# Three kinds of small DMA leave SyncE's queue for ScalarE's and GpSimd's in a two-branch streaming attention layer

## The chip, the cores and the metric

The kernel runs on one core of one Trainium2 chip. The metric is the device time of one execution in microseconds (us); the time of a kernel is the median of its runs. The engines are written as in the profile: PE is TensorE (matmuls; PEld its weight loads), DVE is VectorE, ACT is ScalarE, POOL is GpSimd, SP is SyncE. SP, ACT and POOL can issue DMAs, each from its own queue of instructions, which it works off in order. Each engine waits at an instruction until what it needs from others is there, and what stands behind that instruction on the same engine waits too.

## The reference

One layer of a streaming encoder for 2048 prompt rows and 8 x 16 sample rows (with 512 cached positions each), in float32. Two token mixers work side by side on the same normalised and modulated rows `h`:

```python
qa, ka, va, za, qb, kb, vb, zb, ga, gb = split(h @ w_in)     # 1024 -> 6144
qa, ka = rope(qa), rope(ka)                                  # branch A: 4 heads x 2 x 64
w  = softmax(qa1 ka1') - lam * softmax(qa2 ka2')             # differential attention, chunk-causal mask
oa = w @ va
z  = qb kb' / 8                                              # branch B: 8 heads x 64
a  = sigmoid(z) * exp(reverse exclusive cumsum of log sigmoid(-z))   # stick-breaking attention
ob = a @ vb
ya = (rms_norm(oa) * silu(za)) @ w_branch_a;  yb = (ob * silu(zb)) @ w_branch_b
y  = rms_norm(x + gate * ((sigmoid(ga) * ya + sigmoid(gb) * yb) @ w_out))
```

Besides y for both groups of rows, the outputs are the new keys (of A after rotation) and values of both branches.

## The kernel before

Rows are worked in 17 tiles of 128: prompt tiles 0 to 15 and the sample tile, which the code calls `t == NT`. Products run in float16 pairs: a number is split into a high and a low half, and three of the four products are added up. The work has three stages.

*Start* (to about 200 us in the trace): the modulation, the norm, and `h` transposed, kept in DRAM as `hT_d`.

*Streaming* (to about 1800 us): eight units, alternately a head of A and a pair of heads of B (`kind` 0 and 1). For each unit, `project` (L407) runs over the 17 tiles: 24 matmuls (L428) of the tile's `h`, which SP loads one step ahead (L405), against the unit's weights. `finish` (L438) then evacuates the result. In branch A ACT copies it to `pr` (L442); POOL rotates q and k in three operations (L469, L471, L474) with cosines and sines from a small table `rope`, which `start` (L413) loads for the tile (L423); ACT and DVE split q, k and v into halves. Then come the stores of the tile's k (L484: `rot` in A, `pr` in B), its v (L485) and, in A, of z (L488). `scores` (L625) makes the scores of one tile of queries against all tiles before it. In A the softmax pair is exponentials on ACT and combinations on DVE (L558, L603). In B ACT makes sigmoids, DVE a running product from the right (the scan, L616), POOL multiplies the two (L622, in `stick_weights`), and `turn` (L565) lets ACT write the high half (L572) and DVE the low half (L573; in A L290 and L295). SP then turns the weights with a DMA transpose (L580) into `wt`. Two steps later `pv` (L703) multiplies `wt` with the values (L696 to L698 in A, L700 and L701 in B). `natural` (L669) evacuates the sum to the tile `o`: in A one ACT operation (L675), in B one of ACT (L680), one of DVE (L681) and, for prompt tiles, one of POOL (L683). `store` (L686) adds up the squares of an output of A on ACT (L272) and stores `o` to `o_d[t]` in DRAM (L690).

Into these steps the code interleaves projections for later tiles (about five steps ahead), preparation of the next unit's weights, and norms of caches and weights loaded for that only (L848).

*End* (from about 1800 us): `inputs` (L1168) loads `o_d`, `z_d` and `g_d` tile by tile for the two branch products, the merge and the output product; attention of the sample rows runs beside it and ends in the same `natural` and `store`.

Before the change nearly every DMA is issued by SP (`load` is SP's `dma_start`); ACT issues nine small loads at the start and POOL none. The order of instructions on each engine is not that of the code: the framework lays it out when the program is built, by a simulated timeline of all engines and queues (`schedule_with_timeline_sim=True`), and the chip works it off as laid out. The pools that matter here: `rope`, `rot` and `o` have two buffers each, `wt` five.

Of the kernel before, what the change touches and what calls it, by code (L numbers as in the profile page):

```python
# [25 lines left out]
P = 128  # L26
# [6 lines left out]
NT = SEQ // P  # L33
# [76 lines left out]
def layer_kernel(ctx: ExitStack, tc: tile.TileContext, a: dict):  # L110
    nc = tc.nc
    V, S, G, T = nc.vector, nc.scalar, nc.gpsimd, nc.tensor
    load = nc.sync.dma_start
# [43 lines left out]
    def out_rows(name, t, lo, n):  # L157
        p, s = outs[name]
        return p[t * P : (t + 1) * P, lo : lo + n] if t < NT else s[:, lo : lo + n]
# [3 lines left out]
    o_d = [dram.tile([P, D], F32, name=f"o_d{t}") for t in range(NT + 1)]  # L163
# [23 lines left out]
    def bank(tag, dt=F32):  # L187
        return ps.tile([P, 512 if dt == F32 else 1024], dt, tag=tag, name=f"ps_{tag}", bufs=BANKS[tag])
# [78 lines left out]
    def sum_squares(src, n, dst, width=1024, scale=1.0):  # L267

        for i in range(0, n, width):
            junk = tiny.tile([P, width], F16, tag="junk", name="junk", bufs=1)  # L270
            w = min(width, n - i)
            S.activation(out=junk[:, 0:w], in_=src[:, i : i + w], func=AF.Square, scale=scale,  # L272
                         accum_out=dst[:, i // width : i // width + 1])
# [13 lines left out]
    def split(hi, lo, src, s, on=None):  # L287

        if on is S:
            S.activation(out=hi, in_=src, func=AF.Identity, scale=s)  # L290
        elif on is G:
            G.tensor_scalar(out=hi, in0=src, scalar1=s, scalar2=0.0, op0=ALU.mult, op1=ALU.add)
        else:
            V.tensor_scalar(out=hi, in0=src, scalar1=s, scalar2=None, op0=ALU.mult)
        V.scalar_tensor_tensor(out=lo, in0=src, scalar=s, in1=hi, op0=ALU.mult, op1=ALU.subtract)  # L295
# [106 lines left out]
    def fetch_h(u, t):  # L402
        ahead[u, t] = hs[len(fetched) % 3].bitcast(F16).rearrange("p (f k n) -> p f k n", f=2, n=P)
        fetched.append(t)
        load(out=ahead[u, t], in_=hT_d[t // 4][:, t % 4, :, :, :])  # L405

    def project(U, t):  # L407

        kind, h, sc, sq = U["kind"], U["h"], U["sc"], U["sq"]
        g, i = t // 4, t % 4  # L410
        box = {}

        def start():  # L413
            if t in at_hand:
                box["h"] = at_hand.pop(t)
            else:
                if (U["u"], t) not in ahead:
                    fetch_h(U["u"], t)
                box["h"] = ahead.pop((U["u"], t))
            box["p"] = bank("mm")  # L420
            if kind == 0:
                box["r"] = stg.tile([P, 96], F32, tag="rope", name="rope")
                load(out=box["r"], in_=a["shapes"][:, t * 96 : t * 96 + 96])  # L423

        def mm(n):
            hi, wi = ((0, 0), (0, 1), (1, 0))[n % 3]
# [3 lines left out]
        def piece(n):  # L430
            if n == 0:
                start()
            for j in range(2 * n, 2 * n + 2):
                mm(j)
            if n == 11:
                finish()

        def finish():  # L438
            p, s2, s = box["p"], sc[:, 2:3], sq[:, 0:1]
            pr = stg.tile([P, 512], F32, tag="pr", name="pr", bufs=3)  # L440
            if kind == 0:
                S.activation(out=pr, in_=p, func=AF.Identity, scale=sc[:, 1:2])  # L442
            elif t == NT:
                S.activation(out=pr[:, P:512], in_=p[:, P:512], func=AF.Identity, scale=sc[:, 1:2])
            else:
                S.activation(out=pr[:, P:384], in_=p[:, P:384], func=AF.Identity, scale=sc[:, 1:2])

                assert t % len(rings) not in silu_z
                silu_z[t % len(rings)] = rings[t % len(rings)]
                S.activation(out=rings[t % len(rings)], in_=p[:, 384:512], func=AF.Identity, scale=sc[:, 1:2])  # L450

            qb = qbuf[t % len(qbuf)]
            k16 = stg.tile([P, 2, 2, 64], F16, tag="k16", name="k16")
            vt = kvp.tile([P, 2, 2, 64], F16, tag="v", name="v", bufs=V_BUFS)

            def halves(dst, src, scale):
                src = src.rearrange("p (c d) -> p c d", d=64)
                split(dst[:, :, 0, :], dst[:, :, 1, :], src, scale, S)

            def query(src, scale):  # L460
                src = src.rearrange("p (c d) -> p c d", d=64)
                S.activation(out=qb[:, 0, :, :, :], in_=src.unsqueeze(2).to_broadcast([P, 2, 2, 64]), func=AF.Identity, scale=scale)
                V.scalar_tensor_tensor(out=qb[:, 1, :, 0, :], in0=src, scalar=scale, in1=qb[:, 0, :, 0, :], op0=ALU.mult, op1=ALU.subtract)  # L463
            if kind == 0:
                cosT, sinT = box["r"][:, 0:32], box["r"][:, 32:96]
                x4 = pr[:, 0:256].rearrange("p (c f d) -> p c f d", c=4, f=2)
                rot = stg.tile([P, 256], F32, tag="rot", name="rot")
                r2 = stg.tile([P, 256], F32, tag="r2", name="r2", bufs=1)
                G.tensor_tensor(out=rot.rearrange("p (c f d) -> p c f d", c=4, f=2), in0=x4,  # L469
                                in1=cosT.unsqueeze(1).unsqueeze(1).to_broadcast([P, 4, 2, 32]), op=ALU.mult)  # L470
                G.tensor_tensor(out=r2.rearrange("p (c f d) -> p c f d", c=4, f=2), in0=x4[:, :, ::-1, :],  # L471
                                in1=sinT.rearrange("p (f d) -> p f d", f=2).unsqueeze(1).to_broadcast([P, 4, 2, 32]),
                                op=ALU.mult)
                G.tensor_tensor(out=rot, in0=rot, in1=r2, op=ALU.add)  # L474
                halves(vt, p[:, 256:384], s2)
                query(rot[:, 0:128], s)
                halves(k16, rot[:, 128:256], s)
            else:
                rot = pr
                halves(vt, p[:, 256:384], s2)  # L480
                halves(k16, p[:, 128:256], s2)
                query(p[:, 0:128], s2)
            nk, nv = ("ak", "av") if kind == 0 else ("bk", "bv")
            load(out=out_rows(nk, t, h * P, P), in_=rot[:, 128:256])  # L484
            load(out=out_rows(nv, t, h * P, P), in_=pr[:, 256:384])  # L485
            ui = (h + 4 * kind) * P
            if kind == 0 or t == NT:
                load(out=z_d[t][:, ui : ui + P], in_=pr[:, 384:512])  # L488
            U["v"][t] = vt
            if t == NT:  # L490
                load(out=s_d[U["u"]][:, 6:8, :], in_=vt.rearrange("p c f d -> p c (f d)"))
            U["q16", t], U["k16", t] = qb, k16
# [193 lines left out]
    def store(U, t, o):  # L686
        ui = (U["h"] + 4 * U["kind"]) * P
        if U["kind"] == 0:
            sum_squares(o, P, osums[:, t, U["h"] : U["h"] + 1])
        load(out=o_d[t][:, ui : ui + P], in_=o)  # L690

    def pv_block(job, seg, po, wj, vt, first, last):

# [9 lines left out]
    def pv(job):  # L703

        U, t, c = job["U"], job["t"], job["c"]
        segs = job["segs"] if U["kind"] == 0 else job["segs"][::-1]
        order = [(seg, j) for seg in segs for j in range(seg["hi"] - seg["lo"])]

        def block(i):
            seg, j = order[i]  # L710
            if i == 0 and (U["kind"] == 0 or c == 0):
                U["po", t] = bank("o")
            pv_block(job, seg, U["po", t], j, U["v"][seg["lo"] + j], i == 0, i == len(order) - 1)
            if i == len(order) - 1 and (U["kind"] == 0 or c == 1):
                store(U, t, natural(U, t, U.pop(("po", t))))

        return [(1.5, lambda i=i: block(i)) for i in range(len(order))]
# [4 lines left out]
    def sample(U, dec, qpad, cs):  # L722
# [85 lines left out]
        def finish():  # L808
            po = bank("s")
            vn = box["s"][:, 6:8, :].rearrange("p c (f d) -> p c f d", f=2)  # L810
            for job in box["jobs"]:
                pv_block(job, job["segs"][0], po, 4, vn, True, True)
            o = natural(U, t, po, dec)
            pt = bank("t")
            T.transpose(pt[:, 0:P], box["ot"], ident)
            V.tensor_tensor(out=o, in0=o, in1=pt[:, 0:P], op=ALU.add)
            store(U, t, o)
# [430 lines left out]
    for n in range(len(steps) + PV_LAG):  # L1248
        made, qk, vs = [], [], []
        if n < len(steps):  # L1250
            u, t = steps[n]
# [175 lines left out]
```

## Time and profile before

| | us |
|---|---|
| median of 3 runs | 2351.17 (2347.64 to 2351.97) |
| the profiled execution | 2338.96 |
| its span, first to last instruction | 2337.1 |
| granted TensorE clock in it, mean | 0.965 |
| PE / DVE / ACT / POOL busy | 2121.6 / 1707.5 / 1663.1 / 661.3 |

A row of the profile that names an instruction gives its source line, engine, operation and the tiles it writes and reads (`out<-in`). In the table of waits, `PE ps_o L700 <- DMA wt<-sc_n` reads: PE stood idle before its instruction of L700, which writes `ps_o`, until a DMA from `sc_n` to `wt` had landed; then come the total in us, how often, and the longest. An engine's letter with a `q` (SPq, ACTq) is its sequencer issuing a DMA; its duration is the issue, not the transfer. In the timeline a row begins with start and duration in us, and a bracket holds the idle time before it. The table of stretches gives the length, the busy time of PE, PEld, DVE, ACT and POOL with the number of their instructions, the granted clock, the busy share of the DMA engines and GB/s.

### The profile page before, as it was taken

What the parts mean: (1) busy time and instruction counts of PE and PEld (TensorE: products, weight loads), DVE (VectorE), ACT (ScalarE), POOL (GpSimd) and SP (SyncE); (2) the same over time, 40 slices, a digit from 0 to 9 for tenths busy, and PEclk for the clock granted to TensorE, in tenths of its full rate; (3) what the DMA queues carried; (4) which work ended last, traced back from release to release, by engine and by line L of the source; (5) the groups of instructions that cost most, each with busy time, mean ns of one, the idle gap of its engine ahead of it and who ended that gap; (6) DMA issues with size and microseconds to landing.
All of it is one profiled execution on the core that took longest, in us unless ns stands there. A gap on an engine that the chain in (4) does not pass through costs nothing. (4 is left out here: it accounts for less than half of the span.)

```text
span 2337.1 us, 42708 instructions
## 1 busy us (share of the span) xinstructions
PE 2121.6 (91%) x15272; PEld 1144.0 (49%) x15272; DVE 1707.5 (73%) x3653; ACT 1663.1 (71%) x3292; POOL 661.3 (28%) x578
## 2 busy tenths in 40 slices
PE   5998898998989899899999979999995878989998
PEld 3654454545545445445545545554553444544443
DVE  4658765779875677978667797777788777777663
ACT  4968777787877778778677777866777656756541
POOL 1222022356300334731024474103345111121111
PEclk7999999999999999999999999999997988999999
DMA  9777659897895898867577777756677999999521
GB/s 333 275 214 180 152 118 272 179 193 168 212 210 126 216 204 192 179 178 192 134 191 176 185 168 186 195 146 150 146 171 166 285 254 233 257 245 236 155 98 53
DMA packets 834358, 445.35 MB, mean 191 GB/s; under 512 B 537210, under 2 KB 777130, under 8 KB 833632
## 3 DMA queue, kind: packets, MB, share of 16 engines
q1 hardware_dynamic: 833196, 442.24, 76.0%
q8 instruction: 119, 1.95, 0.4%
q14 instruction: 95, 0.78, 0.1%
q10 hardware_dynamic: 948, 0.39, 0.1%
HBM read 245.60 MB, written 69.24 MB: 135 GB/s over the span
## 5 line engine op out<-in xcount | busy, mean ns | idle before, releaser
L622 POOL TENSOR_TENSOR sc_p<-sc_p,sc_n 128x127 f32<-128x127 f32 (+7 forms) x192 | 313.8, 1638 | 826.5 <-DVE sc_n L616 812.2
L428 PE MATMUL ps_mm<-wb,hs 128*128 128x512 f16 x1632 | 414.5, 382 | 1.5 <-DMA hs<-hT_d 1.3
L428 PEld LDWEIGHTS <-hs 128*128 128x128 f16 x3120 | 274.4, 98 | 257.3 <-DMA hs<-hT_d 11.8
L428 PE MATMUL ps_mm<-wa,hs 128*128 128x512 f16 x1488 | 374.6, 382 | 9.8 <-DVE qbuf L463 6.4
L616 DVE TENSOR_TENSOR_SCAN sc_n<-ps_s,sc_n,zero_t 128x512 f32<-128x512 f32 x192 | 245.4, 1278 | 68.4 <-ACT ps_s L119 65.0
L639 PE MATMUL ps_s<-k,qst 128*128 128x512 f16 (+3 forms) x640 | 224.2, 351 | 37.9 <-DVE sc_n L616 29.9
L573 DVE TENSOR_TENSOR sc_n<-sc_p,sc_n 128x128 f16<-128x128 f32 (+7 forms) x192 | 212.7, 1112 | 58.1 <-ACT sc_n L572 57.6
L504 PEld LDWEIGHTS <-hs 128*128 128x128 f16 x1632 | 156.6, 98 | 188.3 <-ACT qst L532 6.2
L119 ACT ACTIVATE sc_p<-ps_s,usc 128x512 f32<-128x512 f32 (+3 forms) x320 | 204.8, 640 | 30.2 <-PE ps_s L640 25.3
L640 PE MATMUL ps_s<-k,qst 128*128 128x512 f16 (+3 forms) x640 | 224.2, 352 | 0.0
L572 ACT CAST sc_n<-sc_p 128x128 f16<-128x128 f32 (+7 forms) x192 | 155.5, 813 | 78.5 <-POOL sc_p L622 76.9
L700 PE MATMUL ps_o<-v,wt 128*128 128x128 f16 x1088 | 171.5, 225 | 32.6 <-DMA wt<-sc_n 32.2
L119 ACT ACTIVATE ps_s<-ps_s,usc 128x512 f32<-128x512 f32 (+3 forms) x328 | 200.0, 610 | 0.0
L504 PE MATMUL ps_t<-wa,hs 128*128 128x512 f16 x816 | 192.9, 383 | 7.6 <-ACT qst L532 6.0
L504 PE MATMUL ps_t<-wb,hs 128*128 128x512 f16 x816 | 191.9, 380 | 1.2 <-DVE qst L532 0.8
L1344 PE MATMUL ps_o<-wo,wb 128*128 128x512 f16 x816 | 186.5, 383 | 4.1 <-ACT wb L1166 4.1
L701 PE MATMUL ps_o<-v,wt 128*128 128x64 f16 x1088 | 157.9, 197 | 0.0
L700 PEld LDWEIGHTS <-wt 128*128 128x128 f16 x1088 | 105.1, 101 | 98.1 <-DMA wt<-sc_n 45.1
L558 DVE TENSOR_SCALAR_CACHE_REDUCE sc_p<-ps_s,usc 128x512 f32<-128x512 f32 (+3 forms) x160 | 106.3, 665 | 42.4 <-PE ps_s L640 31.7
L616 DVE TENSOR_TENSOR_SCAN sc_n<-ps_s,zero_t 128x128 f32<-128x128 f32 (+3 forms) x128 | 104.1, 814 | 44.0 <-ACT ps_s L119 43.4
L558 DVE TENSOR_SCALAR_CACHE_REDUCE sc_n<-ps_s,usc 128x512 f32<-128x512 f32 (+3 forms) x160 | 106.3, 665 | 36.9 <-PE ps_s L640 26.3
L701 PEld LDWEIGHTS <-wt 128*128 128x128 f16 x1088 | 103.1, 100 | 54.3 <-issue 1.1
(360 smaller groups left out, 4493.6 us busy)
## 6 DMA issues: line engine op xcount, KB each, us to landing
hs<-hT_d SPq DMA_DIRECT2D x130, 512.0 KB, 4.2
g_d<-gt SPq DMA_DIRECT2D x68, 256.0 KB, 4.2
wb<-g_d SPq DMA_DIRECT2D x26, 512.0 KB, 4.8
out_dram<-pr SPq DMA_DIRECT2D x204, 64.0 KB, 2.3
o_d<-o SPq DMA_DIRECT2D x136, 64.0 KB, 2.2
hs<-o_d SPq DMA_DIRECT2D x17, 512.0 KB, 5.6
out_dram<-x SPq DMA_DIRECT2D x17, 512.0 KB, 2.8
wide<-in_w_ada_dram SPq DMA_DIRECT2D x8, 1024.0 KB
```

What stands on the lines that cost most here:

```text
L119: i = S.activation(**kw)
L428: T.matmul(box["p"], box["h"][:, hi, k, :], U["w"][k][:, wi, :], start=(n == 0), stop=(n == 3 * KT - 1))
L504: T.matmul(box["g"][:, 0:gw], box["h"][:, hi, k, :], U["wg"][k // per][:, k % per, wi, :], start=(j == 0), stop=(j == 3 * KT - 1))
L558: V.tensor_scalar(out=dst[:, lo : lo + n], in0=p[:, 0:n], scalar1=sc_pos, scalar2=None, op0=ALU.mult, op1=ALU.max, accum_out=job["mx"][:, ...
L573: V.tensor_tensor(out=lo, in0=src, in1=hi, op=ALU.subtract)
L616: V.tensor_tensor_scan(out=dst[:, lo : lo + n][:, ::-1], data0=src[:, 0:n][:, ::-1], data1=zero_t[:, 0:1].to_broadcast([P, n]), initial=fi ...
L622: G.tensor_tensor(out=p[:, 0:m], in0=p[:, 0:m], in1=n[:, 1 : m + 1], op=ALU.mult)
L639: T.matmul(p[:, 0:n], qst[:, c, :], kk[:, c, 0:n], start=True, stop=False)
L640: T.matmul(p[:, 0:n], qst[:, 2 + c, :], kk[:, c, 0:n], start=False, stop=not diag)
L700: T.matmul(po[:, c * P : (c + 1) * P], wt[:, wj, :], vt[:, c, :, :], start=first, stop=False)
L701: T.matmul(po[:, c * P : c * P + 64], wt[:, nb + wj, :], vt[:, c, 0, :], start=False, stop=last)
L1344: T.matmul(po, st["y"][:, yi * 8 + k, :], wo[j * 4 + k // 2][:, wi, k % 2, :], start=(n == 0), stop=(n == 3 * KT - 1))
```

## The change

Three kinds of DMA are issued by other engines; what they copy, and all computation, stays.

- The load of the rotation table of a tile in branch A (L423), 68 in all, is issued by POOL.
- The store of the rotated k of branch A (L484 with `rot`), 68 in all, is issued by POOL. The k of B and all v and z stay with SP.
- The store of a unit's output `o` (L690) is issued by ACT in branch A (64) and by POOL in branch B (64). The 8 of the sample tile stay with SP.

```diff
             if kind == 0:
                 box["r"] = stg.tile([P, 96], F32, tag="rope", name="rope")
-                load(out=box["r"], in_=a["shapes"][:, t * 96 : t * 96 + 96])
+                G.dma_start(out=box["r"], in_=a["shapes"][:, t * 96 : t * 96 + 96])
...
             nk, nv = ("ak", "av") if kind == 0 else ("bk", "bv")
-            load(out=out_rows(nk, t, h * P, P), in_=rot[:, 128:256])
+
+            (G.dma_start if kind == 0 else load)(out=out_rows(nk, t, h * P, P), in_=rot[:, 128:256])
             load(out=out_rows(nv, t, h * P, P), in_=pr[:, 256:384])
...
         if U["kind"] == 0:
             sum_squares(o, P, osums[:, t, U["h"] : U["h"] + 1])
-        load(out=o_d[t][:, ui : ui + P], in_=o)
+        queue = load if t == NT else S.dma_start if U["kind"] == 0 else G.dma_start
+        queue(out=o_d[t][:, ui : ui + P], in_=o)
```

## The prediction

> **What bounds the kernel now.** I read the page's first part, then TensorE's (PE's) waits, then SyncE's (SP's) own waits and issues, then stretches of the timeline, and last the stages. The profiled execution took 2338.96 us, 1.86 us more than its span; the median of the runs shown is 2351.17 us, 12.2 us above it. I work the change out in us of the span and put it on the median.
>
> ```profile
> span 2337.1 us, 42708 instructions
> PE 2121.6 (91%) x15272; PEld 1144.0 (49%) x15272; DVE 1707.5 (73%) x3653; ACT 1663.1 (71%) x3292; POOL 661.3 (28%) x578
> ```
>
> PE is busy in 91% of the span, so the kernel is bound by PE wherever PE has work, and a gain must be idle time of PE. What ends that idle time and has to do with a DMA is mostly `wt`, the weights turned by a DMA transpose (L580) that SP issues:
>
> ```profile
> PE ps_o L700 <- DMA wt<-sc_n: 32.2, 25, 4.8
> PE ps_o L696 <- DMA wt<-sc_n: 20.4, 14, 4.2
> PE ps_s L639 <- DVE sc_n L616: 29.9, 43, 2.5
> ```
>
> The columns are us in total, times, longest. PE waits 52.6 us in 39 places for `wt`; that is the ceiling of what a freer SP can give by this road (2.3%). The third row is the scan of VectorE (DVE) in branch B, which no queue changes.
>
> SP is one queue in order. Its issues, with duration in ns (min/median/max):
>
> ```profile
> L580 SPq DMA_TRANSPOSE wt<-sc_n x288: 1167/1768/5439, 148.1 to 1798.6; - x144
> L423 SPq DMA_DIRECT2D rope<-in_shapes_dram x68: 332/422/1771, 42.7 to 1471.3; - x68
> L484 SPq DMA_DIRECT2D out_dram<-rot x68: 337/382/1213, 65.9 to 1489.5; - x68
> L690 SPq DMA_DIRECT2D o_d<-o x136: 319/386/3044, 157.9 to 2222.9; - x136
> SPq L690 <- ACT o L675: 34.8, 19, 6.4
> SPq L690 <- POOL o L683: 30.8, 20, 4.9
> SPq L484 <- POOL rot L474: 16.0, 18, 2.4
> ```
>
> 288 transposes by 1.77 us hold SP for about 509 us. The moved copies are 68 tables, 68 rotated k and 128 of the 136 outputs (the sample tile's 8 stay): 68 x 0.42 + 68 x 0.38 + 128 x 0.39 = 104 us of issue. And SP stood 81.6 us at their makers (last three rows) with everything behind it held. So the queue is loaded, but most of its load stays.
>
> **What leaves SP's queue.** How much of PE's 52.6 us hangs on the moved copies I took from the timeline: for each of the 39 waits I went back to the transpose that ended it, took the time from the end of the DVE instruction that made its data to its issue, and in that stretch the moved copies with the waits ahead of them. In 13 of the 39 there was one. The first, one in the middle with three, and the last:
>
> ```profile
> 204.74 0.45 SPq L690 DMA_DIRECT2D o_d<-o  x1
> 205.28 3.37 SPq L580 DMA_TRANSPOSE wt<-sc_n  x1
> 210.83 0.29 PE L696 MATMUL ps_o<-v,wt 128*128 128x128 f16 x1 [2.22 <-DMA wt<-sc_n]
> ...
> 657.67 1.28 DVE L295 SCALAR_TENSOR_TENSOR sc_n<-sc_p,r,sc_n 128x1024 f16<-128x1024 f32 x1
> 659.75 0.51 SPq L690 DMA_DIRECT2D o_d<-o  x1
> 661.42 1.17 SPq L423 DMA_DIRECT2D rope<-in_shapes_dram  x1
> 664.70 0.40 SPq L690 DMA_DIRECT2D o_d<-o  x1
> 665.19 3.84 SPq L580 DMA_TRANSPOSE wt<-sc_n  x2
> 670.11 0.23 PE L696 MATMUL ps_o<-v,wt 128*128 128x128 f16 x1 [1.98 <-DMA wt<-sc_n]
> ...
> 1794.48 1.21 DVE L573 TENSOR_TENSOR sc_n<-sc_p,sc_n 128x1024 f16<-128x1024 f32 x1
> 1796.46 4.40 SPq L580 DMA_TRANSPOSE wt<-sc_n  x2
> 1800.95 0.29 PE L700 MATMUL ps_o<-v,wt 128*128 128x128 f16 x1 [4.85 <-DMA wt<-sc_n]
> ```
>
> At 204.74 one output (0.45 us and the gaps) stands before the transpose: 0.54 us earlier without it. In the middle the data were there at 658.95, the transposes went out at 665.19, and three moved copies took 2.33 us of that; PE waited 1.98, so 1.98 counts. Taking in each place the smaller of the two, the 13 give 8.9 us (0.05 to 1.98 each, the last 0.67). In the other 26 the data themselves were late, or other transposes, loads and stores stood in front. So this term is **-8.9 us**, if each transpose lands as much earlier as it is issued earlier; it is 0 if landing is held by the transfers before it, and no more than -52.6.
>
> **ScalarE's (ACT's) queue** takes 64 outputs of A. Each is issued behind L675, which makes the tile, and the sum of squares that reads it, both ACT's own, so it waits for no other engine. ACT issued copies before only at the start:
>
> ```profile
> L958 ACTq DMA_DIRECT2D wide<-in_lambda_q_dram x2: 352/538/723, 2.7 to 3.7; - x2
> 620.00:900.00 280.00, 262.43 (x1789) 140.19 (x1788) 193.86 (x416) 216.04 (x465) 60.64 (x56) 0.99 0.81 188
> 1010.00:1290.00 280.00, 268.65 (x1830) 143.78 (x1829) 200.41 (x463) 209.71 (x458) 67.63 (x65) 0.99 0.73 176
> 1410.00:1690.00 280.00, 270.62 (x1859) 145.89 (x1858) 211.66 (x497) 200.78 (x445) 71.35 (x71) 1.00 0.66 165
> ```
>
> The last three rows are the stretches that hold most of branch A (columns after the length: PE, PEld, DVE, ACT, POOL busy, clock, DMA share, GB/s). At SP's 0.39 us the 64 cost 25 us of ACT, at a transpose's 1.77 us (an issue held behind one) 113 us. ACT is idle 64 + 70 + 79 = 213 us in these three stretches, while PE is at 94 to 97%. Behind an issue stand ACT's evacuations and exponentials; their lateness is hidden by that idle time, so I take **0**, and 25 us would be the price with the cover gone. A gain is excluded: ACT only gets work.
>
> **GpSimd's (POOL's) queue** takes 200: 68 tables, 68 rotated k, 64 outputs of B. None waits for another engine's compute: L474 and L683 make the k and the output on POOL itself, and the table's buffer is freed by L471, also POOL's. What changes is that a table's load now stands behind whatever POOL waits at, and that L622 (A's rotations too) stands behind issues:
>
> ```profile
> POOL sc_p L622 <- DVE sc_n L616: 812.2, 143, 97.0
> ACT sc_n L572 <- POOL sc_p L622: 76.9, 75, 3.6
> DVE sc_n L573 <- ACT sc_n L572: 57.6, 50, 3.9
> 500.00:620.00 120.00, 109.54 (x817) 60.09 (x816) 110.04 (x218) 96.25 (x207) 73.56 (x64) 0.99 0.81 183
> 900.00:1010.00 110.00, 97.31 (x776) 53.76 (x774) 96.31 (x162) 88.51 (x183) 64.61 (x52) 1.00 0.83 184
> 1290.00:1410.00 120.00, 106.79 (x832) 58.55 (x831) 104.59 (x153) 96.10 (x189) 67.63 (x50) 0.99 0.80 177
> ```
>
> Of the 192 L622, 143 begin when the scan lets them: an issue ahead of these falls into POOL's idle time and is free. 49 (26%) do not. From L622 the lateness goes to ACT's L572 and, in 50 of 192 cases (26%), on to DVE, which is 87 to 92% busy in the three stretches of the last rows, the ends of a B unit with the next unit's A projections beside them. By their places on SP, 74 of the 200 copies fall there (32, 24 and 18; tables, k and outputs by the timeline). 74 x 0.26 x 0.26 = 5.0 issues reach DVE. No row shows what POOL's issue takes. From below it is SP's 0.39 us: 2.0 us; from above a transpose's 1.77 us: 8.9 us, or 20 us if not 26% but POOL's busy share of these stretches, 205.8 of 350 us (59%), is hit (74 x 0.59 x 0.26 = 11.4 issues). I take **+2.0**, as the moved copies' own rows (same tile, same bytes) are the nearest. In the stretches of A above POOL is 22 to 26% busy and hides its part.
>
> The table's load has a price of its own where it comes to stand behind the same waiting L622 as the rotation that reads it. Then POOL waits for a landing:
>
> ```profile
> rope<-in_shapes_dram SPq DMA_DIRECT2D x68, 48.0 KB, 2.4
> ```
>
> 28 tables fall into the three B ends: 28 x 2.4 x 0.26 = 17 us if all did and a quarter reached DVE. The table has two buffers and is loaded at a projection's first piece, its rotation follows the last, so I take 0.
>
> The Trainium skill speaks against POOL's part: its page "SBUF — State Buffer", section "SBUF: two separate sides", says that GpSimd writes the descriptors of its DMAs itself and can't while VectorE runs an op in a mode that holds the port they share. DVE's long rows here are scans out of PSUM and ops of two tensors, which the same page does not count among the modes, so by this rule I would add nothing; no DMA of POOL is in this trace to test it.
>
> **The sum** is -8.9 + 0 + 2.0 = -6.9 us: 2344 us on the median. About 0.2% (4.7 us) is what a measurement of this kernel can tell from no change, so the step is just outside. Its own range is 2338 to 2347.
>
> **The rivals.**
> - *Hidden anyway* (no change, 2347 to 2355). The moved copies only make room in which the transposes wait for each other, or for a landing. For it: the transposes alone are 509 us of issue, and 26 of the 39 waits have no moved copy in front. With half of the 8.9 us realised and the 2.0 paid, it is -2.4: 2349 us. The Trainium skill, "DMA: Bandwidth & Descriptors", section "Issuing engines are not separate DMA queues", states that all queues run on the same DMA engines and that several issuers save only issue time, usually small; by it this rival would be the rule.
> - *GpSimd becomes the late link* (slower). Place: the three B ends above. Price: 11.4 issues x t; at 1.77 us 20 us, less the 8.9 gained: +11, 2362 us, or 2371 with nothing gained. From t = 0.78 us it eats the gain, from 1.2 us the kernel is slower by over 0.2%. Against it: POOL's idle time there is 46.4, 45.4 and 52.4 us, into which 32, 24 and 18 issues fit up to 1.45, 1.9 and 2.9 us each.
> - *A larger gain.* SP's order is not the code's but laid out beforehand from an estimated timeline:
>
> ```profile
> 999.52 0.53 SPq L485 DMA_DIRECT2D out_dram<-pr  x1
> 1002.56 0.38 SPq L484 DMA_DIRECT2D out_dram<-rot  x1
> ```
>
> In the code L484 comes first. With 264 copies gone the layout of every queue is new. If half of the 52.6 us goes, that is -26: 2325 us. The new layout can also lose: PE is idle 38 us in the three stretches of A and 36 in the three B ends, and a fifth more of these 75 us is +15, with the -6.9 it is +8: 2359 us.
>
> **How the numbers follow.** Forecast 0.38, larger gain 0.14, hidden 0.25, GpSimd late 0.16, a worse layout 0.07. Faster by over 0.2%: 0.38 + 0.14 = 0.52; within: 0.25; slower: 0.16 + 0.07 = 0.23. The range goes from 2320 (most of the larger gain) to 2365 (most of GpSimd's price); I leave out about 0.1 on each side.
>
> **What would show it.** Right: SP's waits at L690 for ACT and POOL (65.6 us) and at L484 for POOL (16.0) gone; PE's waits for `wt` down from 52.6 to about 44 us; ACT's waits for L622 not over 85 us; POOL's issues under 0.8 us. Wrong: POOL's issues over 1 us with ACT's and DVE's waits behind L622 up by tens of us; PE's waits for `wt` unchanged although SP is freer; a new wait of POOL's L471 for its table; or differences spread over all engines without a link to the moved copies, which would be the layout.

## The result and the profile after

The kernel after takes 2362.96 us (median of 7 runs, 2355.45 to 2368.18), the kernel before beside it 2347.64 (7 runs, 2342.01 to 2352.07): a ratio of 1.0061 with a 95% interval of 1.0047 to 1.0076. The change makes the kernel slower by 0.6%, 15 us; forecast was 2344 us and faster, the range reached to 2365. The profiled execution after took 2366.43 us, near its median; that of before (2338.96) lies 9 us under its own, so the two profiles differ by 27 us where the medians differ by 15.

The first part of the page after, span and busy times:

```profile
span 2364.6 us, 42426 instructions
PE 2132.6 (90%) x15272; PEld 1150.4 (49%) x15272; DVE 1714.0 (72%) x3653; ACT 1663.8 (70%) x3292; POOL 761.1 (32%) x778
```

POOL has 200 instructions more and is busy 100 us longer: its issues count as work, about 0.5 us each. The queues (packets, MB, share of 16 engines):

```profile
q1 hardware_dynamic: 795180, 426.03, 73.7%
q0 software_dynamic: 6400, 12.01, 2.0%
q10 hardware_dynamic: 10164, 4.58, 0.8%
```

About 16 MB have gone from SP's q1 to q0 (POOL) and q10 (ACT). The moved issues, with ns min/median/max and first and last start (the diff adds one line above L485 and another above L690; before's L484 and L690 are L485 and L692 here):

```profile
L423 POOL DMA_DIRECT2D rope<-in_shapes_dram x68: 545/590/712, 1.3 to 1470.3; - x68
...
L485 POOL DMA_DIRECT2D out_dram<-rot x68: 537/540/586, 67.0 to 1489.7; - x68
...
L692 ACTq DMA_DIRECT2D o_d<-o x64: 326/326/362, 158.7 to 1592.6; - x64
L692 POOL DMA_DIRECT2D o_d<-o x64: 537/578/588, 336.6 to 1821.1; - x64
```

POOL's issue takes 0.54 to 0.59 us, below the 0.78 us that the prediction set as its limit. PE's longest waits after:

```profile
PE ps_o L702 <- DMA wt<-sc_n: 37.5, 23, 7.0
PE ps_o L698 <- DMA wt<-sc_n: 26.3, 19, 3.2
PE ps_s L640 <- DVE sc_n L617: 21.6, 32, 2.9
PE ps_t L805 <- DMA dwt<-dsc: 19.9, 4, 11.1
```

The waits for `wt` (first two rows) are 63.8 us where before had 52.6 and the forecast 44. The last row, from the attention of the sample rows in the end stage, has doubled (9.5 us before), and no moved copy lies there. SP's waits after:

```profile
SPq L581 <- DVE sc_n L574: 128.3, 60, 7.7
...
SPq L486 <- ACT v L290: 72.0, 37, 7.0
...
SPq L485 <- ACT pr L446: 58.8, 24, 6.6
```

and the same three before:

```profile
SPq L580 <- DVE sc_n L573: 74.5, 51, 4.0
...
SPq L484 <- ACT pr L446: 41.6, 19, 6.0
...
SPq L485 <- ACT v L290: 40.5, 28, 5.7
```

SP's waits for the makers of `rot` and `o` are gone, as foretold. In their place SP stands longer for the data of its transposes and stores: 259 us in these three rows where it was 157. It arrives earlier and finds nothing to send. ACT's wait behind L622, which the prediction's slower rival wanted up by tens of us, went down:

```profile
ACT sc_n L573 <- POOL sc_p L623: 68.8, 55, 4.1
```

### The profile page after: what moved, and what is told of

The parts are those of the page before. It is cut to its first block, busy times and chain, and to the rows that moved or that the text cites. A ratio compares the mean times of both kernels' runs of the same rounds, so it can differ in the third digit from the quotient of the medians.

```text
span 2364.6 us, 42426 instructions
## 1 busy us (share of the span) xinstructions
PE 2132.6 (90%) x15272; PEld 1150.4 (49%) x15272; DVE 1714.0 (72%) x3653; ACT 1663.8 (70%) x3292; POOL 761.1 (32%) x778
## 3 DMA queue, kind: packets, MB, share of 16 engines
q8 instruction: 119, 1.95, 0.4%
## 5 line engine op out<-in xcount | busy, mean ns | idle before, releaser
L623 POOL TENSOR_TENSOR sc_p<-sc_p,sc_n 128x127 f32<-128x127 f32 (+7 forms) x192 | 305.4, 1593 | 766.4 <-DVE sc_n L617 760.4
L428 PE MATMUL ps_mm<-wa,hs 128*128 128x512 f16 x1488 | 369.8, 380 | 5.3 <-DMA hs<-hT_d 3.0
L617 DVE TENSOR_TENSOR_SCAN sc_n<-ps_s,sc_n,zero_t 128x512 f32<-128x512 f32 x192 | 245.6, 1279 | 68.3 <-ACT ps_s L119 64.2
L574 DVE TENSOR_TENSOR sc_n<-sc_p,sc_n 128x128 f16<-128x128 f32 (+7 forms) x192 | 218.2, 1141 | 48.5 <-ACT sc_n L573 48.3
L573 ACT CAST sc_n<-sc_p 128x128 f16<-128x128 f32 (+7 forms) x192 | 155.3, 810 | 69.4 <-POOL sc_p L623 68.8
L1346 PEld LDWEIGHTS <-wb 128*128 128x128 f16 x816 | 79.7, 100 | 107.3 <-issue 14.4
```

What stands on the lines that cost most here:

```text
L428: T.matmul(box["p"], box["h"][:, hi, k, :], U["w"][k][:, wi, :], start=(n == 0), stop=(n == 3 * KT - 1))
L573: S.copy(out=hi, in_=src)
L574: V.tensor_tensor(out=lo, in0=src, in1=hi, op=ALU.subtract)
L617: V.tensor_tensor_scan(out=dst[:, lo : lo + n][:, ::-1], data0=src[:, 0:n][:, ::-1], data1=zero_t[:, 0:1].to_broadcast([P, n]), initial=fi ...
L623: G.tensor_tensor(out=p[:, 0:m], in0=p[:, 0:m], in1=n[:, 1 : m + 1], op=ALU.mult)
L1346: T.matmul(po, st["y"][:, yi * 8 + k, :], wo[j * 4 + k // 2][:, wi, k % 2, :], start=(n == 0), stop=(n == 3 * KT - 1))
```

## The experiments

**How order and queue were taken apart.** The framework lays out every engine's order anew when a queue changes. Counted in the two traces, at 6567 of the 15272 places in PE's row of matmuls another one stands after the change (by line, tiles and shape), and at 2077 of DVE's 3653. So nearly all kernels below are built twice: once with one set of queues, to read the order of every engine, SP's other DMAs included; then with another set, each instruction tied behind its predecessor in the first order on its engine, without a wait. Only the moved copies find their places freely. In short form:

```diff
+    nc, _, _, names = built(first)
+    order = [(x.name, x.engine) for b in nc.m.functions[0].blocks for x in b.instructions if x.name in names]
+    nc, arrays, _, names = built(second, order)
...
+                    if str(x.engine) in last:
+                        tc.add_manual_dep(x, last[str(x.engine)], NOSYNC, reason="order")
+                    last[str(x.engine)] = x.name
```

Ratios are to before on the same chip, with 95% intervals. F and T (False and True) say whether a kind moves, in the order tables, rotated k, outputs of A, outputs of B. The traces of the tied kernels show the tied order on every engine. The method by itself, in pin_self:

```diff
+    built([F, F, F, F]); built([F, F, F, F], order)
```

> The kernel before, its own order fixed by the same edges as in the other kernels of this kind, nothing moved: the same program by both theories, 0.9992 to 1.0008. Anything outside is the method's own error, and every ratio of this kind is then read against it.

It gave 0.9994 (0.9981 to 1.0008): no change.

**Queues or order?** Two kernels each keep one half of the change.

pin_queues: before's order, after's queues.

```diff
+    built([F, F, F, F]); built([T, T, T, T], order)
```

> All 264 copies go through the new queues, but every other instruction of every engine stands in exactly the order that it has in the kernel before. Theory Q (the new queues themselves cost the time: GpSimd's issues ahead of its products, ScalarE's ahead of its evacuations): about +14 us on before, as the whole change. Theory L (the queues are worth the few us that were forecast, and the rearranged order of all engines costs the time): -3 to -9 us on before.

pin_layout: after's order, all copies with SP.

```diff
+    built([T, T, T, T]); built([F, F, F, F], order)
```

> The reverse: all copies stay with SyncE, but every engine's other instructions stand in the order of the changed kernel. Theory L: +14 to +24 us on before (the whole loss, and without what the queues give). Theory Q: within 3 us of before.

The queues alone gave 1.0038 (1.0024 to 1.0053), the order alone 1.0024 (1.0009 to 1.0039). Together that is 0.62%, the whole 0.61%: the halves add up, and each is a loss. So neither theory came true: Q wanted the whole with the queues, L a gain there.

**Which order?** Outputs alone were moved with the order left to the framework, then that order was kept and the copies put back on SP.

outA_act:

```diff
-        load(out=o_d[t][:, ui : ui + P], in_=o)
+        (S.dma_start if t < NT and U["kind"] == 0 else load)(out=o_d[t][:, ui : ui + P], in_=o)
```

> Only the 64 outputs of A go through ScalarE's queue; the order is laid out anew. Theory Q: 0 to -3 us, since ScalarE's issues of 0.33 us are hidden. Theory L: anything from -15 to +15 us, without relation to the 64 issues.

outB_pool:

```diff
-        load(out=o_d[t][:, ui : ui + P], in_=o)
+        (G.dma_start if t < NT and U["kind"] == 1 else load)(out=o_d[t][:, ui : ui + P], in_=o)
```

> Only the 64 outputs of B go through GpSimd's queue; the order is laid out anew. Theory Q: this part has the issues that stand ahead of L622, so some +5 us. Theory L: anything from -15 to +15 us, and not the same sign in the end stage, where none of these copies is issued, as a queue would give.

lay_outB and lay_outA, the orders of these two with SP's queue for all:

```diff
+    built([F, F, F, T]); built([F, F, F, F], order)
...
+    built([F, F, T, F]); built([F, F, F, F], order)
```

> The order that is laid out with the outputs of B in GpSimd's queue, but all copies with SyncE. If the order makes the 29 us: +20 to +29 us. If the queue makes them: within 5 us of before.

> The order that arises when only A's outputs go to ScalarE's queue, with all copies back on SyncE's. The kernel with that order and that queue gave 1.0004, and the queue alone, in before's order, 0.9989: if order and queue add up as they did for the whole change, 1.0005 to 1.0025 here. If a re-made order costs about a per cent as a rule, as B's outputs alone did: above 1.005. If orders scatter around before's evenly, below 1 is as likely as above.

| order from | queues of that change | all copies on SP | those queues in before's order |
|---|---|---|---|
| the whole change | 1.0061 (1.0047 to 1.0076) | 1.0024 (1.0009 to 1.0039) | 1.0038 (1.0024 to 1.0053) |
| outputs of B on POOL | 1.0125 (1.0100 to 1.0150) | 1.0134 (1.0114 to 1.0154) | 1.0007 (0.9996 to 1.0019) |
| outputs of A on ACT | 1.0004 (0.9987 to 1.0021) | 1.0034 (1.0017 to 1.0052) | 0.9989 (0.9979 to 1.0000) |

The order alone gives the 29 us that outputs of B cost, within the intervals (four runs each). All three new orders are slower than before's with SP's queue, by 0.24, 1.34 and 0.34%. For outputs of A order and queue together cost less than their product says (1.0023), though the intervals allow it. PE's waits in lay_outB show no single cause:

```profile
PE ps_s L639 <- DVE sc_n L616: 35.9, 40, 2.4
PE ps_o L700 <- DMA wt<-sc_n: 34.4, 19, 5.3
PE ps_t L803 <- DMA dwt<-dsc: 18.7, 3, 11.5
PE ps_o L696 <- DMA wt<-sc_n: 18.1, 18, 3.1
PE ps_mm L428 <- DMA hs<-hT_d: 12.2, 11, 3.8
```

`wt` is at 52.5 where before has 52.6, the scan 6 us above before, and the load of `h` and `dwt` are up; in before the last one was

```profile
PE ps_t L803 <- DMA dwt<-dsc: 9.5, 5, 4.0
```

pin_layout, which has after's order without its queues, shows after's `dwt` wait:

```profile
PE ps_t L803 <- DMA dwt<-dsc: 19.6, 4, 11.8
```

So that row belongs to the order: 18.7 to 19.9 us in three profiles with new orders, 9.5 in before's and 12.0 in pin_self's. lay_outA, also a new order, has 10.4, so it is not in all of them.

**Which of the queues?** Theory P (the port): issues on GpSimd lengthen VectorE's ops of two tensors, by pushing GpSimd's own products onto them (so in pin_rot's expectation) or by holding VectorE off themselves (so in pin_memset's), and this reaches PE. Rivals: GpSimd's time, that is L622 and the rotations come later (the prediction's own); or SyncE, which without these copies sends its other transfers at other times. All kernels below have before's order.

pin_rot, pin_outA, pin_outB:

```diff
+    built([F, F, F, F]); built([T, T, F, F], order)
...
+    built([F, F, F, F]); built([F, F, T, F], order)
...
+    built([F, F, F, F]); built([F, F, F, T], order)
```

> Order of the kernel before on every engine; only the 68 tables and 68 rotated k go through GpSimd's queue. Theory P (GpSimd's issues push its products onto VectorE's ops of two tensors, which then run longer): 136 of the 200 issues, most of them at the ends of the B units, so most of the queues' +9 us: +5 to +9 us, with VectorE's long runs up by some 12 us or more. Theory S (the price is spread over all moved copies, ScalarE's too): about half, +4 us.

> Order of the kernel before; only the 64 outputs of A go through ScalarE's queue. Theory P: no issue of GpSimd, so no price; -1 to -4 us from SyncE's relief. Theory S: +2 us.

> Order of the kernel before; only the 64 outputs of B go through GpSimd's queue. The same change laid out anew cost 29 us. Theory P and S: 0 to +5 us here, so that most of those 29 us is the order. Theory B (the outputs of B in GpSimd's queue are what is dear): +20 us or more.

Tables with rotated k cost 1.0025 (1.0010 to 1.0039), outputs of B 1.0007, outputs of A 0.9989. P's 5 to 9 us came in pin_rot, its 12 us of VectorE's time did not: DVE is busy 1715.5 us, 4.5 above pin_self and 8.0 above before. The last was run again:

> The same kernel as the one that moved only A's outputs to ScalarE's queue in before's order (0.9989, interval 0.9979 to 1.0000). A gain of the freer SyncE: 0.998 to 0.9995 again. No gain: 0.9995 to 1.001.

It gave 0.9994 (0.9977 to 1.0010). At best there is 0.1% in it, and it may be nothing; no version here beats before beyond doubt.

The two parts of pin_rot, and everything but the rotated k:

```diff
+    built([F, F, F, F]); built([F, T, F, F], order)    # pin_rotk
...
+    built([F, F, F, F]); built([T, F, F, F], order)    # pin_rope
...
+    built([F, F, F, F]); built([T, F, T, T], order)    # pin_norotk
```

> Order of before; only the 68 rotated k go through GpSimd's queue, the tables stay with SyncE. In the run with both, the eight stretched VectorE instructions all lay beside the issue of a rotated k. If that is the whole price of the two, this one gives it alone: 1.0015 to 1.0035. If the table is the price (a rotation that waits for a landing behind GpSimd's queue), this gives 0.999 to 1.001.

> Order of before; only the 68 tables through GpSimd's queue. Rotated k alone gave 1.0023, both 1.0025: if they add up, 0.999 to 1.001 here. If a GpSimd issue costs wherever it stands, about as much as the rotated k: 1.0015 to 1.003.

> Order of before; the tables through GpSimd's queue, A's outputs through ScalarE's, B's outputs through GpSimd's, only the rotated k stays with SyncE. All four moved gave 1.0038. If the rotated k is the price of the four: 0.999 to 1.0015, and PE's wait at L517 for VectorE's k is back at 11 us. If it is the number of copies moved, whichever they are: 1.002 to 1.0035.

Rotated k gave 1.0023 (1.0009 to 1.0037), tables 1.0024 (1.0013 to 1.0035), all but rotated k 1.0019 (1.0007 to 1.0031). Either of the first two costs what both cost: the expectations of a sum, and of one culprit, both missed. PE's wait for VectorE's k at L517, expected back at 11 us in pin_norotk if k were the price, is 15.9 us there.

*Is it GpSimd's time?* pin_memset leaves all copies with SP and puts two memsets wherever a table or a k was issued on GpSimd in pin_rot:

```diff
+    junk = con.tile([P, 224], F16, tag="junk", name="junk")
...
+    JUNK[:] = [G.memset(junk, 0.0).ins.name for _ in range(272 * MEM[0])]
```

> Order of before on every engine, all copies with SyncE as before; GpSimd gets 272 memsets of 128x224 f16, two at each of the 136 places at which the tables' loads and the rotated k stood on GpSimd in the run that moved those two (each pair about as long as one issue there, 0.57 us, 77 us in all). The memsets write a tile that nothing reads. If what costs there is the time on GpSimd (its rotations and L622 come later, or it stands busy beside VectorE more), this gives the same +0.25% (ratio 1.0015 to 1.0035) and the same 8 to 12 us more of VectorE's long instructions. If what costs is that GpSimd issues a DMA (descriptors written through a port that VectorE then does not get), it gives no change (0.999 to 1.001) and VectorE's instructions last as in before.

The memsets took

```profile
L1401 POOL MEMSET junk<- 128x224 f16 x272 | 77.6, 285 | 11.4
```

as much as the issues in pin_rot (40.0 + 37.1 us), and the time was 0.9995 (0.9978 to 1.0012). GpSimd's time is free at these places; the rival falls for tables and k. Nor does a later landing show: a table lands 3.4 us after GpSimd's issue, but no row of POOL's waits in pin_queues names it.

*Is it SyncE?* pin_drop leaves the 68 stores of A's rotated k out, so that output is not written.

```diff
-            load(out=out_rows(nk, t, h * P, P), in_=rot[:, 128:256])
+            ((lambda **_: nc.get_next_instruction_name()) if MOVE[1] and kind == 0 else load)(out=out_rows(nk, t, h * P, P), in_=rot[:, 128:256])
```

> Order of before on every engine; the 68 stores of branch A's rotated k are left out altogether (that output is not written), no engine issues them. Theory P, the price of the rotated k lies with the engine that issues it: no change or a small gain from the freer SyncE, 0.996 to 1.0003, and PE's wait at L517 for VectorE's k as before (11 us, 16 us with GpSimd's issues). Theory H, SyncE's queue without these copies and their waits is what costs: 1.0015 to 1.0035, although the work is less.

0.9989 (0.9976 to 1.0002): SP without these copies costs nothing. For k, the price lies with the engine that issues it; for the tables this was not tested.

*What does GpSimd's issue do?* The same place in two traces with the same order on PE and DVE. Before, VectorE's two splits of q and k (L463, L295) and POOL beside them:

```profile
523.30 2.09 DVE L463 SCALAR_TENSOR_TENSOR qbuf<-rot,sq,qbuf 128x128 f16<-128x128 f32 x1
525.31 0.81 DVE L295 SCALAR_TENSOR_TENSOR k<-rot,sq,k 128x128 f16<-128x128 f32 x1
...
522.48 2.76 POOL L622 TENSOR_TENSOR sc_p<-sc_p,sc_n 128x1024 f32<-128x1024 f32 x1 [2.08 <-DVE sc_n L616]
525.20 0.77 POOL L469 TENSOR_TENSOR rot<-pr,rope 128x256 f32<-128x256 f32 x1
```

L463 needs 0.34 us where nothing disturbs it (the median of its 68); here it ends 0.15 us after L622. pin_queues, 4.5 us later in its trace:

```profile
527.82 2.09 DVE L463 SCALAR_TENSOR_TENSOR qbuf<-rot,sq,qbuf 128x128 f16<-128x128 f32 x1
529.83 2.04 DVE L295 SCALAR_TENSOR_TENSOR k<-rot,sq,k 128x128 f16<-128x128 f32 x1
...
527.05 2.70 POOL L622 TENSOR_TENSOR sc_p<-sc_p,sc_n 128x1024 f32<-128x1024 f32 x1
529.70 0.58 POOL L484 DMA_DIRECT2D out_dram<-rot  x1
530.30 0.73 POOL L469 TENSOR_TENSOR rot<-pr,rope 128x256 f32<-128x256 f32 x1
530.98 0.73 POOL L471 TENSOR_TENSOR r<-pr,rope 128x256 f32<-128x256 f32 x1
...
531.93 0.28 PE L517 MATMUL ps_t<-id,k 128*128 128x128 f16 x2 [1.95 <-DVE k L295]
```

L295 began 0.13 us into the issue and ended only 0.16 us after L471: 2.04 us in place of 0.81. PE stands 1.95 us for its `k`.

This is not the rule. At the store before it, 14 us earlier in the same trace, GpSimd pauses for 1.2 us behind the issue, and L295 runs inside the issue at its usual length:

```profile
515.97 0.58 POOL L484 DMA_DIRECT2D out_dram<-rot  x1
516.12 0.34 DVE L295 SCALAR_TENSOR_TENSOR k<-rot,sq,k 128x128 f16<-128x128 f32 x1
```

Six traces have before's order and issues on GpSimd. In them 303 of VectorE's ops on two tensors (none in PSUM) begin during an issue. I call an op held if it is longer by over 0.1 us than the fastest tenth of the same op in three traces without such issues. In 234 cases no tensor op of GpSimd follows the issue within 0.08 us, and none is held; in the other 69 one follows at once, and 35 are held. In pin_memset, 20 such ops begin during a memset with a tensor op right behind, and none is held. So it is not the issue alone that holds VectorE off, but, in half of the cases, an issue with GpSimd's next tensor op behind it; why only half, no run shows. GpSimd's tensor ops and VectorE's meet without any issue too, and the issues move them against each other: in before, 177 of the 252 ops that begin during a GpSimd tensor op are held.

The Trainium skill, "SBUF — State Buffer", section "SBUF: two separate sides", calls the pair of ports that GpSimd shares with VectorE an exclusive lock, held for one whole instruction, also against VectorE ops with two inputs in SBUF if GpSimd's op reads SBUF. The trace agrees on which ops are hit: the 177 beside GpSimd's tensor ops, and none of the 66 that begin during a memset, which reads nothing. It differs in length: L295 was kept out through an issue and two more instructions.

Over the whole trace, DVE's busy time parts the fourteen profiles with before's order in two groups. Eight without GpSimd's issues, pin_memset among them, have 1705.1 to 1711.0 us; six with them 1715.2 (tables) to 1728.1 (all). The ends as the pages have them, pin_self and pin_queues:

```profile
PE 2112.7 (90%) x15272; PEld 1138.6 (49%) x15272; DVE 1711.0 (73%) x3653; ACT 1663.0 (71%) x3292; POOL 663.0 (28%) x578
```

```profile
PE 2125.2 (90%) x15272; PEld 1147.6 (49%) x15272; DVE 1728.1 (73%) x3653; ACT 1663.5 (71%) x3292; POOL 762.5 (32%) x778
```

After has 1714.0 and pin_layout, the same order without the queues, 1690.0: 24 us there too. But VectorE's time is not yet a price: outputs of B alone bring it to 1719.8, more than k (1716.5) or tables, and cost nothing clear of zero. What goes with a loss is a longer wait of PE. Its wait for VectorE's k, in pin_self, pin_rotk and pin_queues:

```profile
PE ps_t L517 <- DVE k L295: 11.5, 11, 2.0
```

```profile
PE ps_t L517 <- DVE k L295: 16.1, 11, 3.5
```

```profile
PE ps_t L517 <- DVE k L295: 16.8, 10, 3.5
```

The row is 10.6 to 11.7 us in the eight profiles without GpSimd's issues, 10.7 with outputs of B alone and 13.9 (tables) to 16.8 in the other five. It rose by 4.6 us in pin_rotk, whose loss is 5.4 us (0.23%), and by 5.3 in pin_queues, whose loss is 8.9. That it makes these losses is argued, not shown.

*A rival that stands: the granted clock.* PE's same matmuls keep it busy 2112.7 us in pin_self's profile (mean clock 0.971), 2127.2 in pin_rotk's (0.963), 2125.2 in pin_queues' (0.962). Of the 15.0 us by which pin_rotk's span is longer, PE's idle time holds only 0.5; of pin_queues' 17.8 it holds 5.3. Over all runs behind the ratios the mean clock is 0.9626 in pin_queues and 0.9642 in pin_rotk, with 0.9662 and 0.9665 in before beside them; pin_rope has 0.9664 beside 0.9669 and loses all the same. Whether PE's new waits lower the clock or it differs for another reason, no run tests.

*And ScalarE's issue?* pin_rotact sends tables and rotated k through ScalarE's queue, pin_allact all four kinds.

```diff
-                load(out=box["r"], in_=a["shapes"][:, t * 96 : t * 96 + 96])
+                (S.dma_start if MOVE[0] else load)(out=box["r"], in_=a["shapes"][:, t * 96 : t * 96 + 96])
...
```

> Order of before on every engine; the tables' loads and the rotated k go through ScalarE's queue instead of GpSimd's (the run with GpSimd's gave 1.0025). Theory of the GpSimd issue that holds VectorE: no issue on GpSimd, so no change or the small gain of a freer SyncE, 0.998 to 1.0005, and VectorE's instructions as long as in before. Rival, the copies' place does not matter, only that they leave SyncE's order or land in another queue: again 1.0015 to 1.0035.

> Order of before; all 264 moved copies go through ScalarE's queue, none through GpSimd's. Theory of the GpSimd issue: the loss is gone and what a freer SyncE brings is left: the outputs of A alone gave 0.9989, so 0.996 to 0.9995; the prediction's own term for the freer SyncE, 8.9 us, would be 0.9962. If ScalarE's 264 issues at about 0.35 us (92 us more on it) reach the path through its softmax work, 1.001 to 1.004.

1.0027 (1.0011 to 1.0043) and 1.0014 (1.0002 to 1.0026). P's expectation missed: no issue on GpSimd, DVE's busy time as in before (1708.5 and 1707.5), PE's wait at L517 11.2 us, and still a loss. ScalarE seems to have a price of its own, a wait that SP had before. In pin_rotact ACT's waits hold two rows that pin_self lacks:

```profile
ACT k L290 <- POOL rot L474: 7.2, 2, 5.1
...
ACT sc_p L119 <- POOL rot L474: 2.5, 1, 2.5
```

The store of the rotated k waits on ACT for POOL's L474, and the exponentials and copies behind it wait with it. PE's waits for `wt` are 63.4 us in pin_rotact, 55.0 in pin_self; pin_rope, without issues on ACT, has 64.2. That these waits of ACT cause all of the 0.27% was not tested.

## Why the prediction was wrong, step by step

- *SP's queue, -8.9 us.* Not realised as a whole. The quarter of it that could be measured alone (outputs of A, 0.9989 and 0.9994; rotated k left out, 0.9989) fits its proportional share of 0.1% and also fits nothing. PE's waits for `wt` never came near 44 us: 51.1 in pin_drop, 53.2 in pin_outA_again, 57.0 in pin_queues, 64.8 in pin_allact, which takes all 264 copies off SP and none to GpSimd. A freer SP waits for the data instead: in the same order it stands 564 us before the transposes of L580 in pin_self and 685 in pin_queues.
- *ACT's 64 outputs, 0.* Right, and for the reason given: each is issued behind ACT's own work. Where that reason is missing (tables and rotated k, pin_rotact) the same queue costs 0.27%.
- *POOL's 200 issues, +2.0 us.* This step failed. The price of one issue was near: with 0.58 us the term is 5.0 x 0.58 = 2.9. The road was wrong. It ran from L622 over ACT to DVE; in before's order ACT's wait behind L622 rose by 4.5 us (79.0 in pin_self, 83.5 in pin_queues), but DVE's behind ACT, the last link, fell from 57.5 to 54.8. (The 68.8 of after belongs to the order: pin_layout has 69.3.) What grew instead is DVE's busy time, 1728.1 us for 1711.0, in its ops of two tensors, and PE's wait for one of them at L517, 16.8 us for 11.5. The prediction had the shared port in hand, saw no row to test it, and added nothing. The queues measured +0.38% (8.9 us) where the sum said -6.9.
- *The rival "GpSimd becomes the late link"* had the sign and, as far as two profiles show it, the place in two of three, not the mechanism. With before's order each matmul has its twin: pin_queues falls from 7.3 to 11.2 us behind pin_self between 500 and 620 us, and from 13.1 to 18.3 between 900 and 1000, the first two B ends (13.5 again at 1075); the third adds nothing (12.8 at 1290, 12.4 at 1450). The 7.3 us ahead of the first end say nothing: pin_outA, without issues on GpSimd and without a loss, is 7.2 behind there. It gains nothing in the two ends (6.9 at 620; 12.0 at 900, 12.4 at 1000).
- *A worse layout*, 0.07, is the other half, which the sum left at nothing: +0.24%, 5.6 us, of the same sign as the +15 that the rival priced and about a third of it; no link to the moved copies was found. The prediction took a new order for a side case with a gain as the likelier outcome; of three, none gained.

**What stays open.** By which road the tables reach PE: L517 rose by 2.4 us only, DVE by 4, of a loss of 5.6. Why the parts don't add up (0.23 and 0.24 give 0.25 together). When an issue with GpSimd work behind it holds VectorE off and when not. What part the lower clock has. Why the new orders lose: their waits are spread, and no edge was tested alone.

## What to carry to other kernels

Before a DMA leaves a busy queue, ask for each copy what the new issuer would wait for and what stands behind it there: a copy whose maker is the issuer itself (outputs of A on ACT) was free, copies that wait for another engine (tables and rotated k on ACT) cost 0.27%, and issues on GpSimd lengthened VectorE's work, at a price (0.23 and 0.24%) or without a clear one (0.07%). Freeing a queue pays only where its data are ready and waiting; rows in which the queue itself stands for data say that they are not. If a planner lays out the order, moving one DMA changes thousands of places: fix the order to see what the move itself does.

## What the runs showed of the hardware

- A GpSimd issue of a 64 KB store takes 0.54 to 0.58 us of the engine (median), of a 48 KB load 0.59; ScalarE's issue of the store takes 0.33, SyncE's 0.38 before.
- A VectorE op with two inputs in SBUF that begins during such an issue runs as usual if GpSimd has no tensor op right behind (0 of 234 longer), and may be kept out if it has (35 of 69): 2.04 us for 0.81 at 529.83 us, over an issue and two tensor ops. 272 memsets with the same total time on GpSimd kept nothing out.
- A table loaded through GpSimd's queue landed 3.4 us after its issue (3.6 in pin_rot), through SyncE's 2.4 in before's profile and 3.0 in pin_rotk's.
